# Two-layer hybrid attention backbone: load order at the start, modulation pace, kept output parts and late C heads

## The chip, the core and the metric

The kernel runs on one core of one Trainium2 chip. The metric is the device time of one execution in microseconds. The engines are TensorE (PE, whose weight loads are listed as PEld), VectorE (DVE), ScalarE (ACT), GpSimd (POOL) and SyncE (SP). Nearly all transfers are issued from SP's queue; ScalarE issues none, and GpSimd issues some small ones. The whole program is planned at build time: each engine gets one fixed list of instructions, with semaphores between the engines.

## The reference

Two layers work on 512 latent tokens `x` and 256 context tokens `ctx`, with a model width D of 2048, all in float32. In each layer (cut to what matters):

```python
shift, scale, gate = split(silu(c) @ w_ada[l] + b_ada[l], 3)          # and the same with c_ctx for ctx
h  = rms(x,  norm_w[l]) * (1 + scale)   + shift
hc = rms(xc, norm_w[l]) * (1 + scale_c) + shift_c
u  = h @ w_in[l]          # queries, keys, values of A and B; low-rank cq, ckv, kpe of C; gate path z
o_a = neighbourhood attention, 8 heads of 64, over latent neighbours and all context keys
o_b = sliding-window grouped attention, 12 query heads, 4 kv heads of 64, with sinks and rotary
o_c = latent attention, 6 heads of 128 + 64, over all 768 keys
y   = concat(o_a, o_b, o_c) * silu(z)
x   = x + gate * (y @ w_out[l])
# layer 0 alone: xc = xc + gate_c * (y_c @ w_out[l]), where context reads context only
```

The output is `x` after the second layer.

## The kernel before

**Precision and tiles.** Every float32 operand of a data matmul is split in a high part (float32r) and a low rest, and three products are made: high by high, high by low, low by high. The splitter (L394) does it for weights: a ScalarE copy to `wh`, then a VectorE subtraction to `wl`. `hilo` (L343) does it for activations. There are 3 buffers of `ws` (weights as loaded), 3 of `wh`, 2 of `wl`, 6 PSUM banks `g`, one double bank `S`, 5 buffers `tm`, and 52 buffers `s3` of 128 x 768 (named `s` in the profile) for nearly everything else.

**The planner.** Strands of work are Python generators (fibers) with priorities. `Weaver.run` (L111) runs them against a virtual clock, with a cost for each instruction (L230 to L337), and so fixes the order of each engine's list. `main` goes through a list of jobs; a `TJob` (L437) or `FJob` (L538) makes one output tile column by pieces of weights, and spawns a `post` strand that empties its PSUM banks. A job with `fine` waits for its inputs slice by slice (128 rows of K, called k). A `Group` deals the pieces of several jobs by turns. A strand that needs an event or a buffer that is not there yields to others.

**The start.** `load_x` (L874) loads the rows of x and of ctx as 24 tiles of 128 x 512 from SP's queue: for each of four column blocks, four of x, then two of ctx. `use_x` and `turn_x` square and transpose them. `ada_blocks` (L724) then streams the shift and scale columns of `w_ada` of layer 0 through PE; after its first eight loads it sets `ev_go`, with which the weight loader begins. The first eight loads are the shift and scale columns of k = 0. `make_hk` (L951) forms h for slice k as soon as its shift and scale are there. Layer 0's first jobs are `kv` and `q` of four A heads, their K halved by `HALF`, in one Group.

**The rest of modulation.** All other modulation vectors (gate of layer 0, shift, scale and gate of layer 1) are made on VectorE by `ada_vec` (L784): for each slice of 128 x 512 of `w_ada`, loaded to one of two `wa` buffers, one multiply-add into `ac` for each of latent and context (L266), then a small PE reduction. After each slice the strand sleeps `PACE[stage[0]]` planner microseconds (L814): 5.5 at first, 2.0 from the last C weight job of layer 0 on (`stage` 1, L2124), 10.0 from layer 1 on. Gate 0 and layer 1's shift and scale are 192 slices of two products; gate 1 is 64 slices of one. The gates go to DRAM (`gscr`) and come back as rows, one for all partitions.

**Order in a layer.** A heads, B heads, then the C heads, mixed with jobs of z and of the low-rank parts; attention units (scores, softmax, transposes, value product) are run by two worker strands beside the jobs. The C heads come last, in the order of `ORDER_C`. A head's gated output is stored to DRAM (`yscr`) and, by `load_y` (L1939) and `load_one` (L1950), loaded back and split for the output projection; L1939 waits until enough `s3` buffers are free.

**Output projection.** The first `CUT` output columns blocks of 256 (3 in layer 0, 2 in layer 1) are cut in K: a job over k = 0 to 13 whose result is kept by `post_part` (L1965), and later a finishing job over k = 14 and 15 whose `post_out` (L1978) adds the kept part, multiplies by the gate, adds the residual x, and in layer 0 also squares for the next norm. The other columns are one job each, the later ones 512 wide; in layer 1 `post_out` then multiplies, adds and stores to the output.

Of the kernel before, what the change touches and what calls it, by code (L numbers as in the profile page):

```python
# [21 lines left out]
D = 2048  # L22
# [19 lines left out]

HALF = 8
# [4 lines left out]
PACE = [5.5, 2.0, 10.0]  # L48
# [91 lines left out]
class Kern:  # L140
# [296 lines left out]
class TJob:  # L437


    def __init__(self, K, W, runs, nk, tiles, lhs, evs, post, room=None, kpp=2, after=None, k0=0):  # L440
        self.after, self.np, self.k0 = after, nk // kpp, k0
        self.K, self.W, self.runs, self.nk, self.tiles, self.kpp = K, W, runs, nk, tiles, kpp
        self.lhs, self.evs, self.post, self.room = lhs, evs, post, room
        self.wd = sum(n for _, n in runs)
        m = 512 // self.wd
        self.banks = [tiles[i:i + m] for i in range(0, len(tiles), m)]
        self.ps = [None] * len(self.banks)
        self.done = [Event() for _ in self.banks]
        self.inS = self.fine = False

    def specs(self):
        n, m = self.wd, self.kpp

        def mk(p):
# [8 lines left out]
            return dict(load=load, kind="split", cols=m * n)  # L463
# [168 lines left out]
def body(K):  # L632
# [241 lines left out]
    def load_x():  # L874

        for c in range(4):
            st = []
            for i in range(6):
                x = yield from K.get("s3")
                w.cur.ft = w.vt  # L880
                src = t["x"][0, i * 128:(i + 1) * 128] if i < 4 else t["ctx"][0, i * 128 - 512:i * 128 - 384]
                tx = yield from K.load_ahead(x[:, :512], src[:, c * 512:(c + 1) * 512])
                st.append((x, tx))
            w.spawn(use_x(c, st), 0)

    def use_x(c, st):
        left = [4, 4]
        for k in range(4 * c, 4 * c + 4):
            xk[k] = yield from K.get("s3")
        for k in range(4 * c, 4 * c + 4):  # L890
            for seg in range(2):
                w.spawn(turn_x(k, seg, st, left), 1)
        sq = yield from K.get("s3")
        for i, (x, tx) in enumerate(st):
# [3 lines left out]
        for e in ev_x[c]:  # L898
            K.set(e)

    def turn_x(k, seg, st, left):
        a, b = SEG[seg]
        w.cur.ft = max(tx for _, tx in st[a:b])
# [8 lines left out]
        if left[seg] == 0:  # L912
            K.put("s3", *(x for x, _ in st[a:b]))
# [496 lines left out]
    def layer(l):  # L1410
# [473 lines left out]
        def attend_C(h):  # L1884
# [54 lines left out]
        def load_y():  # L1939
            for f in range(KT):  # L1940
# [4 lines left out]
                s = yield from K.get("s3", n=3)  # L1945
                hi, lo = K.take("s3", F32R), K.take("s3", F32R)
# [3 lines left out]
        def load_one(f, s, hi, lo):  # L1950
            yield from K.load(s[:, :ntok], yscr[f], 512 * ntok)
# [12 lines left out]

        def post_part(n):  # L1965

            def gen(ps, done):
                for b in range(len(qt) // 2):
# [3 lines left out]
                    K.put("g", ps[b])  # L1972
                    K.set(ev_part[n, b])
            return gen
# [3 lines left out]
        def post_out(c0, wd, tiles):  # L1978
# [8 lines left out]
            def gen(ps, done):  # L1987
# [3 lines left out]
                gs, tg, xin = {}, 0.0, []  # L1991
                for x in sides:
                    if x == 0 or wd > 256 or 0 not in sides:
                        g = yield from K.get("tm")
                    gs[x] = (g, 256 * x if wd == 256 else 0)
                    ga = gscr[l][x]
                    yield from K.load(g[:, gs[x][1]:gs[x][1] + wd], bass.AP(tensor=ga.tensor, offset=ga.offset + c0, ap=[[0, 128], [1, wd]]),
                           512 * wd)
# [10 lines left out]
                for b, ts in enumerate(banks):  # L2009
                    yield from K.wait(done[b])  # L2010
                    xt, tx = xin[b] if early else ((yield from K.get("tm")), None)
# [3 lines left out]
                    w.cur.ft = w.vt  # L2015
                    r = slice(ts[0] % 4 * 128, ts[0] % 4 * 128 + 128 * m)
                    if not early:
                        if ts[0] < 4:
                            src = (xs1 if last else t["x"][0])[r, cols]
                        else:  # L2020
                            src = t["ctx"][0, r, cols]
                        yield from K.load(xv, src.rearrange("(t p) n -> p t n", p=128))
                        tx = w.cur.ft
                    w.cur.ft = max(done[b].t, tg)
                    src = ps[b]
                    if (c0 // 256, b) in part:
                        yield from K.wait(ev_part[c0 // 256, b])
                        yield from K.add(o, src, part[c0 // 256, b][:, :512])
                        K.put("s3", part[c0 // 256, b])
                        src = o  # L2030
                    g, ga = gs[int(ts[0] >= 4)]
                    yield from K.mul(ov, src.rearrange("p (t n) -> p t n", n=wd),
                          g[:, None, ga:ga + wd].to_broadcast([128, m, wd]))
# [9 lines left out]
                    K.put("s3" if early else "tm", xt)  # L2043
# [33 lines left out]
        if cut:  # L2077
# [4 lines left out]
            jobs.extend([Group([kv[0], q[0]]), Group(zs), Group([kv[1], q[1]]), zjob(0)])  # L2082
# [23 lines left out]
        jobs[-1].after = free_h  # L2106
        J(lambda: w.spawn(free_B(), 1))
# [15 lines left out]
        if l == 0:  # L2123
            J(lambda: stage.__setitem__(0, 1))  # L2124
        J(lambda: free_c("kv", 4))

        def free_y(kpp):
# [3 lines left out]
            return fn  # L2131

# [6 lines left out]
        while c0 < D:  # L2139
            wd = 512 if c0 % 512 == 0 else 256  # L2140
            final = c0 + wd == D
            for tiles in ([lat, cx] if final and not last else [qt]):
# [3 lines left out]
                jobs.append(TJob(K, t["w_out"][l], [(c0, wd)], KT, tiles, lhs_y, ev_yT, post_out(c0, wd, tiles), kpp=kpp,  # L2146
                                 after=free_y(kpp) if final and tiles[-1] == qt[-1] else None))
                jobs[-1].inS = wd == 512 and tiles is not cx
            c0 += wd
# [48 lines left out]
    def ada_rest():  # L2198
# [3 lines left out]
        stage[0] = 2  # L2202
# [72 lines left out]
```

## Time and profile before

| | us |
|---|---|
| runs of the kernel before | 2886.25, 2877.25, 2882.88 |
| their median | 2882.88 |
| the profiled execution's own time | 2875.56 |
| its span, first to last instruction | 2873.8 |

The mean granted TensorE clock of the profiled execution is 0.992. The profile is of one execution, with times counted from the span's start. Windows give each engine's busy time in a stretch; a tile is named by the program's name for it. L233 is every ScalarE activation, L239 every VectorE two-tensor instruction, L266 every VectorE scalar-tensor-tensor instruction, L277 the softmax maximum, L308 every load and store from SP's queue, L338 every data matmul and L341 every transpose, because helpers record them; so groups are told apart by their tiles. PE idle time between matmuls is listed with the engine that ended it.

### The profile page before, as it was taken

The numbers are of one execution on the slowest core, as the hardware profiler recorded it, in microseconds if no ns is written. First come the engines' busy times: TensorE is split into PE (matmuls) and PEld (weight loads), VectorE is DVE, ScalarE is ACT, GpSimd is POOL, SyncE is SP. The second block draws the span as 40 slices with busy tenths as digits, with TensorE's granted clock in tenths as the row PEclk, the third lists the DMA queues.
The fourth block names the chain that finished last, engine by engine and source line by source line (L and its number), as shares of the span: only waits on it lengthen the run. The fifth ranks groups of instructions, "written<-read, shape, count | busy, mean of one in ns | idle before, by whom it ended". The sixth has DMA issues, their size and how long they took to land.

```text
span 2873.8 us, 51646 instructions
## 1 busy us (share of the span) xinstructions
PE 2774.4 (97%) x19270; PEld 2610.4 (91%) x19270; DVE 1985.4 (69%) x5088; ACT 1209.1 (42%) x2656; POOL 147.9 (5%) x217
## 2 busy tenths in 40 slices
PE   7999999999999999899999999999999999999998
PEld 5789999999999999889988779999999888889977
DVE  4347776757897688989873485656667867599643
ACT  3323434434444354556321273433334545466421
POOL 2000000000011001000000000000001000000000
PEclk8999999999999999999999999999999999999999
DMA  9853434333233334325353443333333333413253
GB/s 291 281 166 105 120 92 121 107 103 111 86 99 102 107 111 144 100 81 165 113 169 103 137 149 107 109 105 107 109 107 92 103 115 111 120 46 97 85 177 117
DMA packets 388428, 349.93 MB, mean 122 GB/s; under 512 B 47876, under 2 KB 315954, under 8 KB 388176
## 3 DMA queue, kind: packets, MB, share of 16 engines
q1 hardware_dynamic: 386304, 345.31, 40.2%
q0 software_dynamic: 1872, 1.32, 0.5%
q8 instruction: 151, 2.47, 0.4%
q14 instruction: 101, 0.83, 0.1%
HBM read 305.01 MB, written 32.07 MB: 117 GB/s over the span
## 4 chain that ended last, share of the span: by engine, by line
PE 82%; DVE 10%; DMA 3%; issue 2%; ACT 2%; SPq 1%; DVEq 0%; ACTq 0%
PE g L338 65%; PE S L338 10%; PE g L341 5%; DVE s L239 2%; DVE wl L239 1%; DVE s L266 1%; DVE s L277 1%; PE g L761 1%; DVE ac L266 1%; ACT s L233 1%; PE g L819 1%; DVE tm L239 1%; DVE s L261 1%; DVE pt L239 1%; SPq L308 1%
## 5 line engine op out<-in xcount | busy, mean ns | idle before, releaser
L338 PE MATMUL g<-wh,s 128*128 128x256 f32 (+2 forms) x6248 | 1304.4, 297 | 21.9 <-DVE tm L239 5.6
L338 PEld LDWEIGHTS g<-wh,s 128*128 128x128 f32 x6248 | 1022.8, 192 | 50.1 <-ACT s L233 9.6
L338 PE MATMUL g<-wl,s 128*128 128x256 f32 (+2 forms) x3124 | 920.8, 295 | 5.7 <-DVE wl L239 5.2
L338 PE MATMUL g<-s,wh 128*128 128x384 f32 (+1 forms) x2688 | 762.2, 354 | 1.2 <-ACT s L233 0.8
L239 DVE TENSOR_TENSOR wl<-ws,wh 128x512 fp32r<-128x512 f32 (+1 forms) x606 | 418.2, 690 | 496.0 <-PE g L338 273.2
L338 PEld LDWEIGHTS g<-wl,s 128*128 128x128 f32 x3124 | 599.0, 192 | 20.6 <-DVE wl L239 11.2
L233 ACT ACTIVATE wh<-ws 128x512 fp32r<-128x512 f32 (+2 forms) x614 | 377.6, 616 | 437.3 <-PE g L338 357.0
L338 PEld LDWEIGHTS g<-s,wh 128*128 128x128 f32 x2688 | 492.1, 188 | 31.2 <-issue 2.1
L338 PE MATMUL g<-s,wl 128*128 128x384 f32 (+1 forms) x1280 | 448.2, 350 | 0.3 <-DVE wl L239 0.3
L233 ACT ACTIVATE s<-s,sm 128x512 f32<-128x512 f32 (+3 forms) x260 | 192.5, 740 | 453.8 <-DVE sm L277 369.9
L266 DVE SCALAR_TENSOR_TENSOR ac<-wa,scT,ac 128x512 f32<-128x512 f32 x420 | 307.9, 753 | 5.4 <-DMA wa<-w_ada 4.9
L338 PEld LDWEIGHTS g<-s,wl 128*128 128x128 f32 x1280 | 240.9, 188 | 12.4 <-DVE wl L239 0.6
L341 PE MATMUL g<-ident,s 128*128 128x128 f32 x1488 | 225.4, 279 | 22.8 <-DMA s<-x 6.8
L338 PE MATMUL S<-s,s 128*128 128x256 f32 (+3 forms) x1260 | 233.1, 313 | 12.4 <-DVE sm L277 6.2
L239 DVE TENSOR_TENSOR pt<-g,pt 128x512 fp32r<-128x512 f32 (+1 forms) x306 | 187.2, 622 | 42.6 <-ACT pt L233 40.7
L338 PE MATMUL g<-pt,s 128*128 128x256 f32 (+1 forms) x1348 | 208.4, 285 | 8.2 <-DVE pt L239 5.6
L338 PEld LDWEIGHTS S<-s,s 128*128 128x128 f32 x1260 | 187.6, 189 | 29.8 <-DVE sm L277 12.5
L233 ACT ACTIVATE pt<-g 128x512 fp32r<-128x512 f32 (+1 forms) x306 | 160.1, 542 | 120.4 <-PE g L341 116.2
L341 PEld LDWEIGHTS g<-ident,s 128*128 128x128 f32 x1488 | 176.6, 143 | 35.6 <-issue 8.4
L233 ACT ACTIVATE tm<-g 128x384 f32<-128x384 f32 (+4 forms) x240 | 113.4, 491 | 205.5 <-PE g L338 131.3
L338 PEld LDWEIGHTS g<-pt,s 128*128 128x128 f32 x1348 | 184.5, 191 | 14.5 <-DVE pt L239 8.9
L287 POOL TENSOR_TENSOR s<-ot,s 64x256 f32<-64x256 f32 x100 | 88.1, 881 | 1467.5 <-DVE ot L239 1328.6
(163 smaller groups left out, 2429.3 us busy)
## 6 DMA issues: line engine op xcount, KB each, us to landing
ws<-w_in SPq DMA_DIRECT2D x288, 256.0 KB
wa<-w_ada SPq DMA_DIRECT2D x256, 256.0 KB
ws<-w_out SPq DMA_DIRECT2D x144, 256.0 KB
s<-w_ada SPq DMA_DIRECT2D x128, 256.0 KB
ws<-w_in SPq DMA_DIRECT2D x200, 128.0 KB
s<-scr SPq DMA_DIRECT2D x36, 384.0 KB
ws<-w_qb SPq DMA_DIRECT2D x54, 192.0 KB
s<-scr SPq DMA_DIRECT2D x40, 256.0 KB
```

What stands on the lines that cost most here:

```text
L233: self.nc.scalar.activation(out, in_, func, bias=bias, scale=scale, **kw)
L239: self.nc.vector.tensor_tensor(out, a, b, op=op)
L261: self.nc.vector.tensor_scalar(out, a, s1, s2, op0=op0, op1=op1)
L266: self.nc.vector.scalar_tensor_tensor(out, a, s, b, op0=op0, op1=op1)
L277: self.nc.vector.tensor_tensor_reduce(out, a, b, -1.0, init, OP.add, OP.min, acc)
L287: self.nc.gpsimd.tensor_tensor(out, a, b, op=OP.mult)
L308: self.nc.sync.dma_start(out, in_)
L338: self.nc.tensor.matmul(out, l, r, start=start, stop=stop, skip_group_check=True)
L341: self.nc.tensor.transpose(out, in_, self.ident)
L761: nc.tensor.matmul(ps[j:j + 32, :n], scT[:, kk, :], s[:, x * n:(x + 1) * n], start=kk < 4, stop=kk >= 12, skip_group_check=True)
L819: nc.tensor.matmul(pt[:, 2 * c + m:2 * c + m + 1], a[:, c * 128:(c + 1) * 128], one, start=c == 0 and m == sides[0], stop=c == n // 128 - ...
```

## The change

Six edits are made together.

1. `load_x` loads all 16 tiles of x first. The 8 tiles of ctx wait for `ev_go`, that is for the issue of the first eight modulation loads. `use_x` and `turn_x` work per segment.
2. The first Group of layer 0 has q ahead of kv.
3. The paces become 4.0, 25.0, 2.0 and 10.0 by stage. The new stage 1 begins after the last z job of layer 0, before the C heads; stage 2 begins where stage 1 did; stage 3 is layer 1.
4. C heads with y tile 12 or above (`STAY`) keep their gated output in its buffer; `load_one` splits it from there, with no store and reload.
5. `post_part` multiplies its bank by the gate row and adds the residual when it keeps it; the finishing job's `post_out` then multiplies its own bank by the gate and adds the kept part as its residual.
6. The last output job of layer 1 has its weights multiplied by the gate row in the splitter; `post_out` then only adds and stores. The gate row is loaded by a strand spawned one job ahead.

```diff
-PACE = [5.5, 2.0, 10.0]
+STAY = 12
+PACE = [4.0, 25.0, 2.0, 10.0]
...
 def splitter(self):
+            if sp.get("gate"):
+                yield from self.wait(sp["gate"][1])
+                yield from self.mul(s, s, sp["gate"][0][0])
...
 def load_x():
-        for c in range(4):
-            st = []
-            for i in range(6):
+        for seg in range(2):
+            for c in range(4):
+                if seg:
+                    yield from K.wait(ev_go)
+                st = {}
+                for i in range(*SEG[seg]):
...
 def attend_C(h), use():
-                    yield from K.store(yscr[f], sz[f][:, :ntok], 512 * ntok)
-                    K.put("s3", sz[f])
+                    if f < STAY:
+                        yield from K.store(yscr[f], sz[f][:, :ntok], 512 * ntok)
+                        K.put("s3", sz[f])
...
 def load_y():
-                s = yield from K.get("s3", n=3)
-                hi, lo = K.take("s3", F32R), K.take("s3", F32R)
+                s = (yield from K.get("s3", n=3)) if f < STAY else sz[f]
+                hi = yield from K.get("s3", F32R, n=2)
+                lo = K.take("s3", F32R)
 def load_one(f, s, hi, lo):
-            yield from K.load(s[:, :ntok], yscr[f], 512 * ntok)
+            if f < STAY:
+                yield from K.load(s[:, :ntok], yscr[f], 512 * ntok)
+            else:
+                yield from K.wait(ev_y[f])
...
 def post_part(n), gen(ps, done):
+                yield from K.wait(ev_gate[l])
+                gs = yield from gates(n * 256, 256, range(1 if last else 2))
                 for b in range(len(qt) // 2):
                     yield from K.wait(done[b])
+                    xt = yield from K.get("tm")
+                    yield from K.load(xv, residual(n * 256, 256, [2 * b, 2 * b + 1]))
                     part[n, b] = yield from K.get("s3")
-                    yield from K.act(part[n, b][:, :512], ps[b])
+                    yield from K.mul(o, ps[b], gate row)
                     K.put("g", ps[b])
+                    yield from K.add(o, o, xt)
...
 def post_out(c0, wd, tiles, gated=False), gen(ps, done):
-                    if (c0 // 256, b) in part:
-                        yield from K.add(o, src, part[c0 // 256, b][:, :512])
-                    yield from K.mul(ov, src, gate row)
-                    K.put("g", ps[b])
+                    if not gated:
+                        yield from K.mul(ov, sv, gate row)
+                        K.put("g", ps[b])
+                        sv = ov
                     if last:
-                        yield from K.add(ov, ov, xv)
+                        yield from K.add(ov, sv, xv)
...
-            jobs.extend([Group([kv[0], q[0]]), Group(zs), Group([kv[1], q[1]]), zjob(0)])
+            jobs.extend([Group([q[0], kv[0]]), Group(zs), Group([kv[1], q[1]]), zjob(0)])
...
         for f in range(10 if last else 13, KT):
             jobs.append(zjob(f))
+        if l == 0:
+            J(lambda: stage.__setitem__(0, 1))
...
-            J(lambda: stage.__setitem__(0, 1))
+            J(lambda: stage.__setitem__(0, 2))
...
+                gated = final and last
+                if gated:
+                    jobs.insert(len(jobs) - 1, Call(lambda: w.spawn(load_g(), 1)))
+                    jobs[-1].gate = (gl, ev_gl)
```

In the diff, `gate row` stands for the broadcast slice of the gate tile, and `xv` is the kept part in a finishing job.

More of the change, by code (lines that the diff above doesn't have):

```diff
@@ L448, in __init__ @@
         self.done = [Event() for _ in self.banks]
+        self.gate = None
         self.inS = self.fine = False
@@ L462, in load @@
                     off += wd
-            return dict(load=load, kind="split", cols=m * n)
+            return dict(load=load, kind="split", cols=m * n, gate=self.gate)
         return [mk(p) for p in range(self.nk // m)]
@@ L874, in load_x, with use_x @@
     def load_x():
-        for c in range(4):
-            st = []
-            for i in range(6):
[L879 to L886, printed above, removed]
+        for seg in range(2):
[4 more added lines that the diff above has]
+                for i in range(*SEG[seg]):
+                    x = yield from K.get("s3")
+                    w.cur.ft = w.vt
+                    src = t["ctx"][0, i * 128 - 512:i * 128 - 384] if seg else t["x"][0, i * 128:(i + 1) * 128]
+                    tx = yield from K.load_ahead(x[:, :512], src[:, c * 512:(c + 1) * 512])
+                    st[i] = (x, tx)
+                w.spawn(use_x(c, seg, st), 0)
+    def use_x(c, seg, st):
         left = [4, 4]
         for k in range(4 * c, 4 * c + 4):
[L889 to L892, printed above, removed]
+            if seg == 0:
+                xk[k] = yield from K.get("s3")
+            w.spawn(turn_x(k, seg, st, left), 1)
         sq = yield from K.get("s3")
-        for i, (x, tx) in enumerate(st):
+        for i, (x, tx) in st.items():
             w.cur.ft = max(w.vt, tx)
@@ L912, in turn_x @@
         if left[seg] == 0:
[L913 removed]
+            K.put("s3", *(x for x, _ in st.values()))
         yield from K.copy(xk[k][:, a * 128:b * 128], ps[:, :(b - a) * 128])
@@ L1963, in layer, with residual, gates @@
         part = {}
+        def residual(c0, wd, ts):
+            r = slice(ts[0] % 4 * 128, ts[0] % 4 * 128 + 128 * len(ts))
+            src = t["ctx"][0] if ts[0] >= 4 else xs1 if last else t["x"][0]
+            return src[r, c0:c0 + wd].rearrange("(t p) n -> p t n", p=128)
+        def gates(c0, wd, sides):
+            gs = {}
+            for x in sides:
+                if x == 0 or wd > 256 or 0 not in sides:
+                    g = yield from K.get("tm")
+                gs[x] = (g, 256 * x if wd == 256 else 0)
+                ga = gscr[l][x]
+                yield from K.load(g[:, gs[x][1]:gs[x][1] + wd], bass.AP(tensor=ga.tensor, offset=ga.offset + c0, ap=[[0, 128], [1, wd]]),
+                       512 * wd)
+            return gs
@@ L1990, in gen @@
                 w.cur.ft = w.vt
[L1991 to L1998, printed above, removed]
+                xin = []
+                gs = {} if gated else (yield from gates(c0, wd, sides))
                 tg = w.cur.ft
@@ L2010, in gen @@
                     yield from K.wait(done[b])
-                    xt, tx = xin[b] if early else ((yield from K.get("tm")), None)
+                    cut = part.get((c0 // 256, b)) if wd == 256 else None
+                    if cut is not None:
+                        xt = cut
+                    else:
+                        xt, tx = xin[b] if early else ((yield from K.get("tm")), None)
                     o = yield from K.get("tm")
@@ L2015, in gen @@
                     w.cur.ft = w.vt
-                    r = slice(ts[0] % 4 * 128, ts[0] % 4 * 128 + 128 * m)
[L2017 to L2023, printed above, removed]
-                    w.cur.ft = max(done[b].t, tg)
-                    src = ps[b]
-                    if (c0 // 256, b) in part:
-                        yield from K.wait(ev_part[c0 // 256, b])
-                        yield from K.add(o, src, part[c0 // 256, b][:, :512])
[L2029 to L2033, printed above, removed]
-                    K.put("g", ps[b])
+                    if cut is not None:
+                        yield from K.wait(ev_part[c0 // 256, b])
+                        tx = w.cur.ft
+                    elif not early:
+                        yield from K.load(xv, residual(c0, wd, ts))
+                        tx = w.cur.ft
+                    r = slice(ts[0] % 4 * 128, ts[0] % 4 * 128 + 128 * m)
+                    w.cur.ft = max(done[b].t, tg)
+                    sv = ps[b].rearrange("p (t n) -> p t n", n=wd)
+                    if not gated:
+                        g, ga = gs[int(ts[0] >= 4)]
+                        yield from K.mul(ov, sv, g[:, None, ga:ga + wd].to_broadcast([128, m, wd]))
+                        K.put("g", ps[b])
+                        sv = ov
                     w.cur.ft = max(w.cur.ft, tx)
                     if last:
-                        yield from K.add(ov, ov, xv)
+                        yield from K.add(ov, sv, xv)
+                        if gated:
+                            K.put("g", ps[b])
                         yield from K.store(t["out"][0, r, cols].rearrange("(t p) n -> p t n", p=128), ov)
@@ L2042, in gen @@
                                   ov[:, :, kk * 128:(kk + 1) * 128], xv[:, :, kk * 128:(kk + 1) * 128])
-                    K.put("s3" if early else "tm", xt)
+                    K.put("s3" if early or cut is not None else "tm", xt)
                     K.put("tm", o)
@@ L2131, in free_y, with load_g @@
             return fn
+        gl, ev_gl = [], Event()
+        def load_g():
+            yield from K.wait(ev_gate[l])
+            g = yield from K.get("s3")
+            ga = gscr[l][0]
+            yield from K.load(g[:, :512], bass.AP(tensor=ga.tensor, offset=ga.offset + D - 512, ap=[[0, 128], [1, 512]]))
+            gl.append(g[:, :512])
+            K.set(ev_gl)
         cut = CUT[l]
@@ L2201, in ada_rest @@
         yield from K.wait(*(e for p in ev_in[1] for e in p))
-        stage[0] = 2
+        stage[0] = 3
         yield from ada_gate(1)
```

24 lines of the change are left out of this document (19 added, 5 removed).

## Prediction

> **What bounds the kernel now.** I read the page first, then busy time by windows of the stages, then who TensorE (PE) waited for in the worst stages, then the order of time at both ends.
>
> ```profile
> span 2873.8 us, 51646 instructions
> PE 2774.4 (97%) x19270; PEld 2610.4 (91%) x19270; DVE 1985.4 (69%) x5088; ACT 1209.1 (42%) x2656; POOL 147.9 (5%) x217
> PE 82%; DVE 10%; DMA 3%; issue 2%; ACT 2%; SPq 1%; DVEq 0%; ACTq 0%
> ```
>
> PE is busy 97% and makes 82% of the chain that ended last. No matmul on data is removed here, so only PE's gaps, 2873.8 - 2774.4 = 99 us of them, can be won, and a little at the end. Where they lie (columns: window, its length, PE, PEld, DVE, ACT, POOL busy, granted clock, DMA share, GB/s):
>
> ```profile
> core 0: us, PE busy (x) PEld busy (x) DVE busy (x) ACT busy (x) POOL busy (x), PEclk, DMA share, GB/s
> 0.00:50.00 50.00, 31.31 (x255) 24.48 (x255) 26.03 (x81) 23.07 (x65) 19.46 (x41) 0.83 1.01 269
> 50.00:150.00 100.00, 93.68 (x850) 76.59 (x851) 34.98 (x73) 27.62 (x54) 1.72 (x3) 0.97 0.94 298
> 250.00:1100.00 850.00, 841.41 (x6097) 833.18 (x6096) 647.34 (x1708) 358.75 (x836) 64.77 (x81) 1.00 0.35 104
> 750.00:850.00 100.00, 96.15 (x745) 94.48 (x744) 91.35 (x254) 49.00 (x126) 12.15 (x13) 1.00 0.28 82
> 1100.00:1350.00 250.00, 228.94 (x1567) 216.51 (x1566) 226.31 (x643) 143.21 (x331) 12.11 (x20) 0.99 0.39 119
> 1450.00:1510.00 60.00, 53.12 (x427) 52.19 (x426) 43.99 (x73) 12.09 (x19) 0.00 (x0) 0.97 0.54 164
> 2400.00:2650.00 250.00, 243.88 (x1586) 224.79 (x1586) 198.72 (x578) 142.71 (x326) 5.95 (x6) 1.00 0.32 95
> ```
>
> Three places lose: the start (DMA full, 18.7 us idle in 50), the C heads of layer 0 (1100 to 1350: 21.1 us idle, DVE busy 226 of 250), and the cut output jobs of layer 0 (1450 to 1510: 6.9 us). The C heads of layer 1 (2400 to 2650) do the like with 6.1 us idle. What differs is the modulation, whose products of w_ada tiles (wa) sit on DVE (same columns, only instructions on wa, so DVE alone):
>
> ```profile
> 150.00:1100.00 950.00, 186.00 (x260) 1.00 0.37 109
> 1100.00:1350.00 250.00, 37.05 (x51) 0.99 0.39 119
> 1350.00:1510.00 160.00, 51.46 (x73) 0.99 0.47 147
> ```
>
> One k-slice is two such instructions. To 1100 the planner's pace of 5.5 gave 130 slices in 950 us, 7.3 us each, so 1.8 us over the pace. 384 instructions make gate 0 and all layer-1 vectors: 260 + 51 + 73.
>
> **New paces (4 / 25 / 2 / 10).** At 4.0 plus the same 1.8 a slice takes 5.8 us: 950 / 5.8 = 164 slices by 1100, 34 more than now. These are 68 instructions at 37.05 / 51 = 0.73 us, 50 us of DVE that move from 1100 to 1510 into the A and B stages. Beside C a slice comes every 25 + 1.8 us: 9 slices, 13 us of DVE instead of 37. The 19 slices left run at the old stage's 160 x 2 / 73 = 4.4 us, 84 us, and end near 1430.
>
> C of layer 0 gets 24 us of DVE back. Who is waited for there, then one row of C in layer 1, then the DMA queue in C of layer 0 (us in total, times, longest):
>
> ```profile
> PE g L338 <- DVE pt L239: 4.6, 4, 1.8
> PE g L338 <- DVE wl L239: 4.0, 5, 1.7
> PE g L338 <- ACT wh L233: 2.3, 1, 2.3
> PE S L338 <- DVE sm L277: 2.0, 3, 1.1
> SPq L308 <- DVE ac L266: 12.4, 4, 7.1
> ```
>
> The long waits are for DVE, and SP's queue stands 12.4 us behind wa tiles, with weight loads (ws) queued behind them. With the pause both shrink. The gain is at least about 0 (if gaps are chain latency) and at most 33.5 us, the idle time of the weight-load row (250 - 216.51). I take layer 1's C, the nearest row with no modulation: 2.4% idle; 228.94 / 0.976 = 234.5, so **-16**. DVE then needs 226 - 24 = 202 of 234, 86%, against layer 1's 79%: near enough. Low end of the gain 4, high end 30.
>
> A and B pay: DVE goes from 647 to about 693 of 850 (82%). PE idles 8.6 us there now. The stretch 750 to 850 shows the price of a full DVE: 91% busy, 3.9 us idle in 100. If four further stretches of 100 us come to that, each 3 us worse than the mean of 1, it costs 12; if DVE's slack hides all, 0. The one such stretch that there is lies among eight, and 50 us spread over 850 bring one or two more there: **+4**, ends 0 and 12. The wait queued behind it is the splitter's lo part (wl) and the softmax, which stand behind the two products on DVE.
>
> [...]
>
> **Start.** The eight ctx loads move behind the first eight modulation loads, and q's weights go before kv's. DMA queue, then PE, then the ctx size:
>
> ```profile
> 19.92 2.90 SPq L308 DMA_DIRECT2D s<-ctx  x2
> 22.87 9.54 SPq L308 DMA_DIRECT2D s<-w_ada  x8
> 36.07 5.09 SPq L308 DMA_DIRECT2D s<-w_ada  x7
> 43.36 0.38 PE L338 MATMUL g<-wh,s 128*128 128x256 f32 x1 [1.99 <-ACT s L233]
> 51.10 0.58 PE L338 MATMUL g<-wh,s 128*128 128x256 f32 x1 [1.99 <-ACT s L233]
> s<-ctx SPq DMA_DIRECT2D x8, 256.0 KB
> ```
>
> 2 MB at 269 to 298 GB/s is 7 to 8 us: the first shift and scale columns, and the first projection matmul at 43.36, come that much sooner. But they serve k = 0 alone; the next eight modulation loads now stand behind ctx, so k = 1 (51.10) stays where it is, as the bytes ahead of it are the same. PE's program is in order and bank 0 of the first piece needs k = 1 after six matmuls. Only those and some transposes leave the busy region, so **-2**, ends -8 (all of it) and +3 (ctx late for bank 2 of q, the ctx transposes then beside projections). What is late next is k = 1's modulation, DMA-bound.
>
> **Kept parts.** In layer 0, 3 jobs x 3 banks. Before: ACT copies the part; later DVE adds part, multiplies by the gate, adds x. After: DVE multiplies and adds x when kept, later it multiplies and adds. Waits at 1450 to 1510, DVE groups there, and the ACT copy at 1340 to 1460:
>
> ```profile
> PE g L338 <- DVE tm L239: 5.6, 3, 2.4
> PE g L819 <- DVE tm L239: 1.1, 1, 1.1
> L266 DVE SCALAR_TENSOR_TENSOR ac<-wa,scT,ac 128x512 f32<-128x512 f32 x30 | 21.3, 748 | 3.5 <-DMA wa<-w_ada 3.3
> L239 DVE TENSOR_TENSOR s<-tm 128x256 f32<-128x256 f32 x14 | 5.5, 419 | 1.1 <-DMA tm<-x 1.1
> L239 DVE TENSOR_TENSOR tm<-tm 128x512 f32<-128x512 f32 x7 | 4.8, 689 | 0.2
> L239 DVE TENSOR_TENSOR tm<-g,s 128x512 f32<-128x512 f32 x7 | 4.8, 688 | 0.1
> L271 DVE TENSOR_REDUCE ssx<-s 128x6 f32<-128x768 f32 x3 | 2.8, 944 | 0.0
> L233 ACT ACTIVATE s<-g 128x512 f32<-128x512 f32 x6 | 3.6, 596 | 10.6 <-PE g L338 10.6
> ```
>
> PE waits there for PSUM banks (g) that DVE has not read. A finishing job costs DVE 3 x (0.688 + 0.689 + 2 x 0.419) + 2 x 0.944 = 8.5 us, beside 43% modulation; after, 3 x (0.689 + 0.838) + 1.9 = 6.5 us, the bank is freed by the first instruction, and modulation is over. Of 5.6 + 1.1 = 6.7 us I take **-6**, ends 0 and -7. Early, the parts add 9 x 1.38 = 12 us to DVE, which loses 17 slices there (25 us): nothing, as long as modulation ends by 1450. The product now waits for the gate row and holds its bank meanwhile; the gate's 64 slices are done near 150 + 64 x 5.8 = 521, so only its load can be late, with the softmax of the last heads queued behind it on DVE: 1 or 2 us, in the ends. Nine residual loads and six gate loads go earlier on SP's queue, beside DMA at half load: 0. Layer 1 (4 banks, no modulation, 0 to -2): 0.
>
> The eviction moves from ACT (596 ns) to DVE (688 ns, the same as the 689 ns of an SBUF source). [...]
>
> **Late heads of C on chip.** Four y tiles per layer skip a store and a reload; the loads of y, first and last:
>
> ```profile
> 1306.92 1.46 SPq L308 DMA_DIRECT2D s<-scr  x3
> 1360.32 0.32 SPq L308 DMA_DIRECT2D s<-scr  x1
> ```
>
> The last is needed only by the finishing jobs near 1480, so its trip is hidden: 0. The held tiles take up to four of 52 buffers; that loads began at once after q's buffers fell free says there was room. Ends -3 (less queueing) and +6 (a head's room waits).
>
> **The end.** Layer 1's last job has its weights multiplied by the gate in the splitter: 16 x 0.69 us on DVE, and only an add behind the last matmul.
>
> ```profile
> 2867.17 0.40 PE L338 MATMUL g<-wh,s 128*128 128x512 f32 x1
> 2864.47 0.69 DVE L239 TENSOR_TENSOR tm<-S,tm 128x512 f32<-128x512 f32 x1 [2.88 <-PE S L338]
> 2867.55 0.68 DVE L239 TENSOR_TENSOR tm<-g,tm 128x512 f32<-128x512 f32 x1
> 2869.60 0.69 DVE L239 TENSOR_TENSOR tm<-tm,s 128x512 f32<-128x512 f32 x1
> 2865.91 4.74 SPq L308 DMA_DIRECT2D out_dram<-tm  x4
> ```
>
> DVE ends at 2870.3, 2.7 us behind PE's last matmul, since four banks bring eight instructions. With four, the last add starts some 0.7 us after that matmul's end at 2867.6 at the latest and ends by 2868.4 to 2869: **-2**, ends -1 and -2.2. The products hide beside matmuls: DVE idles 2.88 us before the first row, waiting for PE, and one product fits there. The splitter waits for the gate row, with its own later pieces and the weight buffers behind it; the row is loaded a job ahead. Without that cover the products cost 16 x 0.69 = 11.
>
> **Sum.** -2 + 4 - 16 - 6 + 0 - 2 = -22. The profiled execution took 2875.56 (span 2873.8), so it would be 2853.6; the median of the runs, 2882.88, is 7.3 above it, so I forecast 2882.88 - 22 = **2861**.
>
> **Rivals.**
> 1. C's gaps are latency (softmax chain, split chain), not DVE's load. For it: layer 1's C idles too. Against: DVE at 91%. C gives 4: -10, **2873**. Chance 0.14.
> 2. C nearly closes: 30 instead of 16, as SP's blocking goes too: -36, **2847**. 0.15.
> 3. Slower: DVE becomes the bound in A and B. It decides from about 90% busy; the new mean is 82%. If two thirds of the 850 us run at C's present 8.4% idle, that is 48 us against 6 now, +42 in place of +4: +16, **2899**. For it: 750 to 850 is at 91% already. Against: that stretch idles only 3.9%. 0.08.
> 4. The pace does nothing in A and B (slices stay at 7.3 us, bound by queue or DVE): A and B cost 0, 62 slices are left, 9 go beside C, and 53 x 4.4 = 233 us reach past the cut jobs, so their 6 are lost: -20, **2863**. 0.05.
>
> My forecast has 0.58. What a measurement can tell from no change is 0.3%, 8.6 us. Faster: 0.54 of my case, rivals 2 and 4, half of rival 1, 0.81; within: the rest of both, 0.12; slower 0.07. The range, 2840 to 2879, holds the forecast with the ends of C, A and B, and rivals 1, 2 and 4.
>
> **What would show it.** Right: in 1100 to 1350 under 20 wa instructions, PE idle under 10 us, DVE under 90%; no wa instruction after 1450; no waits on tm at the cut jobs; first projection matmul near 36 but k = 1 near 50; four adds at the end. Wrong: PE idle in 250 to 1100 above 20 us, or PE idle in C still near 20 with DVE lighter.

## The result, and the profile after

The changed kernel takes **2865.72 us** in the median of 4 runs (2865.18 to 2867.86), beside 2883.7 for the kernel before (4 runs, 2877.25 to 2886.25): ratio 0.9948, 95% interval 0.9935 to 0.9961, so 15 us faster by the ratio and 17 below the median that the forecast of 2861 set out from. The sign came out, and two thirds to three quarters of the forecast 22; of the terms behind the size, not all did.

The profiled execution after took 2865.18 us, close to its median. That of before took 2875.56, 7 to 8 below its own: the two traces differ by 10.4 us, and what they are short of the timing lies in no trace.

The page after, its head and the shares of the chain:

```profile
span 2863.4 us, 51590 instructions
PE 2776.1 (97%) x19270; PEld 2616.3 (91%) x19270; DVE 1997.8 (70%) x5113; ACT 1199.0 (42%) x2643; POOL 148.8 (5%) x217
PE 83%; DVE 10%; DMA 3%; issue 2%; ACT 1%; SPq 1%; DVEq 0%; ACTq 0%
```

TensorE still bounds the kernel, with 12 us less idle (2863.4 - 2776.1 = 87 instead of 99). The same windows as in the prediction, with the same columns, after the change:

```profile
0.00:50.00 50.00, 30.63 (x259) 24.02 (x260) 28.45 (x83) 23.69 (x67) 19.51 (x41) 0.86 0.97 281
50.00:150.00 100.00, 96.14 (x876) 79.07 (x876) 35.39 (x76) 26.87 (x53) 1.76 (x3) 0.97 0.96 298
250.00:1100.00 850.00, 837.57 (x6049) 829.05 (x6048) 671.69 (x1728) 350.42 (x824) 67.57 (x81) 0.99 0.38 112
750.00:850.00 100.00, 92.83 (x704) 90.87 (x703) 88.48 (x248) 47.44 (x125) 12.57 (x12) 0.93 0.29 87
1100.00:1350.00 250.00, 236.54 (x1611) 227.00 (x1610) 224.13 (x656) 149.25 (x347) 11.12 (x20) 0.97 0.36 108
1450.00:1510.00 60.00, 59.89 (x500) 59.68 (x499) 30.48 (x54) 13.14 (x20) 0.00 (x0) 1.00 0.41 118
2400.00:2650.00 250.00, 244.28 (x1615) 225.81 (x1614) 203.14 (x581) 145.91 (x333) 4.18 (x5) 1.00 0.30 92
```

C of layer 0 has PE busy 236.5 instead of 228.9, the cut jobs 59.9 instead of 53.1 of 60. The stretch 750 to 850 went the other way: 92.8 instead of 96.2, and the clock fell from 1.00 to 0.93. In C the clock fell too, from 0.99 to 0.97. Windows at fixed times hold slightly different work in the two kernels, so I also use a **lead**: the trace lists every matmul, and adding up their durations at full clock in order gives the work done at each moment; the lead is how much earlier the changed kernel has done the same work. It comes out so, in us (time in the kernel before, lead there):

| 142 | 807 | 861 | 1113 | 1343 | 1446 | 1505 | 2693 | 2745 | 2850 | end |
|---|---|---|---|---|---|---|---|---|---|---|
| +3.0 | +3.5 | -6.3 | -6.0 | +3.8 | +0.8 | +9.7 | +12.4 | +7.2 | +8.8 | +10.4 |

So the start won 3, one place near 815 lost 10, C won 10, the stretch behind it gave 3 back, the cut jobs won 9, layer 1's cut jobs lost 5 and the end won 3. A lead is read from one execution each: in e1, a second run of the same program, the place near 815 lost 7.5, C won 8 and the end stands at +7.3. A single term is thus good to 2 or 3 us.

**The loss near 815.** Waits of PE in 750 to 850 (total, times, longest), the longest before and then after; after the change, PE's rows and DVE's around the wait; then three windows:

```profile
PE g L338 <- DVE pt L239: 1.6, 1, 1.6
PE S L340 <- DVE sm L279: 4.7, 2, 4.1
814.81 0.74 PE L340 MATMUL S<-s,s 128*128 128x256 f32 x4
819.68 1.43 PE L340 MATMUL S<-s,s 128*128 128x384 f32 x4 [4.13 <-DVE sm L279]
814.26 0.48 DVE L279 CUSTOM_DVE_ANT_0 s<-S,zero,sm 128x256 f32<-128x256 f32 x1
819.14 0.48 DVE L279 CUSTOM_DVE_ANT_0 s<-S,zero,sm 128x256 f32<-128x256 f32 x1
800.00:820.00 20.00, 15.87 (x131) 15.63 (x131) 17.05 (x39) 9.22 (x20) 2.27 (x2) 0.94 0.38 112
820.00:840.00 20.00, 17.79 (x103) 16.69 (x103) 14.98 (x45) 10.73 (x34) 1.71 (x2) 0.72 0.18 54
818.00:828.00 10.00, 6.11 (x23) 5.01 (x24) 7.78 (x22) 3.39 (x10) 0.00 (x0) 0.50 0.26 80
```

One matmul waits 4.13 us for a softmax maximum (L279), and the clock then is at 0.50 for 10 us and averages 0.72 over 20 us. From the end of one maximum (814.74) to the end of the next (819.62) DVE takes 4.9 us, with one modulation product of 0.75 us in between, right behind the first maximum. PE's list has no other matmul between these two groups of score products, so it stands idle for most of that chain. The wait costs 4, the lost clock (1 - 0.72) x 20 + (1 - 0.94) x 20 = 6.8 more, together 11, where the lead shows 10. A wait of 4.1 us stands there in every run with the pace of 4.0 (one number, seen in eight profiles), and in none with 4.7 or 5.5.

**The loss in layer 1's cut jobs.** The window 2700 to 2760 before, then after, then the timeline after (SPq is a DMA issue):

```profile
2700.00:2760.00 60.00, 59.13 (x366) 52.89 (x366) 29.24 (x51) 18.48 (x32) 0.00 (x0) 1.00 0.50 152
2700.00:2760.00 60.00, 56.09 (x303) 48.74 (x302) 23.18 (x36) 14.01 (x23) 0.00 (x0) 0.94 0.44 132
2716.33 0.39 SPq L310 DMA_DIRECT2D out_dram<-tm  x1
2720.88 0.69 DVE L241 TENSOR_TENSOR tm<-g,tm 128x512 f32<-128x512 f32 x1 [3.81 <-DMA out_dram<-tm]
2722.69 0.68 DVE L241 TENSOR_TENSOR wl<-ws,wh 128x512 fp32r<-128x512 f32 x1
2723.42 0.80 PE L340 MATMUL S<-wl,s 128*128 128x512 f32 x1 [3.91 <-DVE wl L241]
```

A product with the gate waits 3.81 us for its output tile, because the tile's last content is still on its way to DRAM; the splitter's lo half stands behind it on DVE, PE 3.91 us behind that, and the clock falls: to 0.50 in the 5 us behind that wait (2723.4 to 2728.4), to 0.94 over the 60 us. The parts gated early take tm tiles (five in all) for gate rows and residual rows just before the finishing jobs want theirs; that this is why a tile with an open store comes up here, and not in the kernel before, is my reading of the program and not measured.

### The profile page after: what moved, and what is told of

The parts are those of the page before. It is cut to its first block, busy times and chain, and to the rows that moved or that the text cites. A ratio compares the mean times of both kernels' runs of the same rounds, so it can differ in the third digit from the quotient of the medians.

```text
span 2863.4 us, 51590 instructions
## 1 busy us (share of the span) xinstructions
PE 2776.1 (97%) x19270; PEld 2616.3 (91%) x19270; DVE 1997.8 (70%) x5113; ACT 1199.0 (42%) x2643; POOL 148.8 (5%) x217
## 4 chain that ended last, share of the span: by engine, by line
PE 83%; DVE 10%; DMA 3%; issue 2%; ACT 1%; SPq 1%; DVEq 0%; ACTq 0%
PE g L340 66%; PE S L340 10%; PE g L343 5%; DVE wl L241 1%; DVE s L268 1%; DVE s L241 1%; SPq L310 1%; DVE s L279 1%; DVE tm L241 1%; PE g L825 1%; DVE ac L268 1%; ACT s L235 1%; PE g L767 1%; DVE pt L241 1%; DMA s<-w_ada 1%
## 5 line engine op out<-in xcount | busy, mean ns | idle before, releaser
L340 PEld LDWEIGHTS g<-wl,s 128*128 128x128 f32 x3124 | 599.1, 192 | 21.1 <-DVE wl L241 12.2
L235 ACT ACTIVATE tm<-g 128x384 f32<-128x384 f32 (+3 forms) x240 | 113.0, 490 | 201.6 <-PE g L340 136.3
```

The costliest lines, as they stand in the source:

```text
L235: self.nc.scalar.activation(out, in_, func, bias=bias, scale=scale, **kw)
L340: self.nc.tensor.matmul(out, l, r, start=start, stop=stop, skip_group_check=True)
```

## The experiments

The kernel before had medians of 2882 to 2884 beside them. Intervals are 0.0012 to 0.0016 to either side, some 4 us, so differences of 2 or 3 us between runs settle nothing by themselves, and 5 us barely.

| run | median us | ratio to before | 95% interval |
|---|---|---|---|
| e1, the changed kernel again | 2868.14 | 0.9947 | 0.9935 to 0.9959 |
| e2, old pace | 2867.77 | 0.9950 | 0.9938 to 0.9962 |
| e3, pause only | 2870.51 | 0.9956 | 0.9943 to 0.9968 |
| e4, fast pace only | 2865.2 | 0.9940 | 0.9928 to 0.9951 |
| e5, late heads as before | 2868.55 | 0.9946 | 0.9932 to 0.9960 |
| e6, start as before | 2870.36 | 0.9954 | 0.9943 to 0.9966 |
| e7, last job not gated in its weights | 2872.81 | 0.9964 | 0.9951 to 0.9977 |
| e8, layer 1's parts as before | 2864.22 | 0.9930 | 0.9914 to 0.9946 |
| e9, store from the kept part | 2862.45 | 0.9926 | 0.9913 to 0.9939 |
| e10, e9 with pace 4.7 | 2852.58 | 0.9893 | 0.9879 to 0.9907 |
| e11, layer 0's gated parts alone | 2874.18 | 0.9966 | 0.9952 to 0.9979 |
| e12, e10 without the pause | 2861.55 | 0.9927 | 0.9913 to 0.9941 |

**The paces, e1 to e4.** e1 is the changed kernel itself.

> The changed kernel itself, to see what of its profile comes again. My theory: its one long PE wait in the B stage (4.1 us at 815 us, for the softmax maximum on DVE) and the half clock behind it (0.72 from 820 to 840 us) follow from the order of DVE's list, and so come again, as do the 3.9 us wait near 2718 us and the clock dip behind it; median 2863 to 2869 us. Rival: the clock dips are an accident of one execution; then PE's clock from 800 to 850 us is 1.00 here and the span is 5 to 8 us shorter.

It came out with the same wait of 4.1 us and a clock of 0.95 in 750 to 850, and the same loss near 2718: PE waits 4.1 us there, and the clock is 0.94 over 2700 to 2760. Both waits belong to the program.

```diff
-PACE = [4.0, 25.0, 2.0, 10.0]
+PACE = [5.5, 5.5, 2.0, 10.0]     # e2
+PACE = [5.5, 25.0, 2.0, 10.0]    # e3
+PACE = [4.0, 4.0, 2.0, 10.0]     # e4
```

> Paces of before (5.5 up to the output jobs, then 2.0), all other edits kept. My theory (DVE load decides): A and B get back about 10 us (PE idle 250 to 1100 under 10 us), C loses about 11 (PE idle 1100 to 1350 near 21 us again), the cut jobs lose 5 to 7 since modulation runs beside them; median 2870 to 2876 us. Rival (the paces only shuffle the order, the gain is from the other edits): 2863 to 2868 us.

> Old pace 5.5 before C, pause (25) beside C, then 2.0. My theory: A and B get back about 10 us, C keeps its gain (PE idle 1100 to 1350 near 13 us), but some 53 slices are left behind C, at 4.4 us each about 230 us, so they lie beside the cut jobs and those wait again for tm (5 to 7 us): 2860 to 2866 us. Rival (the cut jobs gain by the gated parts, not by the end of modulation): no waits on tm at the cut jobs, 2853 to 2858 us.

> Pace 4.0 up to and in C, no pause. A and B are the same as in the changed kernel, with the same long wait. My theory: the 28 slices left at 1100 us take 5.8 us each, 160 of C's 250 us, so C loses about two thirds of its gain, 6 to 8 us: 2871 to 2875 us. Rival (C's gaps are latency, not DVE's load): 2864 to 2868 us.

e2 and e4 came out where their rivals had them and not where my theory did (2870 to 2876, 2871 to 2875); e3 is above both of its ranges. The new paces as a whole are worth nothing that can be measured (e2 beside e1). Nor is the pause alone: at 4.0 the kernel without it (e4) is 3 us faster than e1, at 5.5 the one without it (e2) 3 us faster than e3, both within the noise. The window of C, and that of the cut jobs, in e2 and then e4:

```profile
1100.00:1350.00 250.00, 232.20 (x1592) 219.97 (x1591) 226.89 (x649) 145.18 (x340) 12.11 (x20) 0.99 0.38 115
1450.00:1510.00 60.00, 55.70 (x459) 54.89 (x458) 46.98 (x81) 11.99 (x18) 0.00 (x0) 1.00 0.56 164
1100.00:1350.00 250.00, 233.71 (x1623) 222.57 (x1622) 233.99 (x684) 146.83 (x341) 11.70 (x20) 1.00 0.39 119
1450.00:1510.00 60.00, 59.80 (x498) 59.60 (x498) 30.03 (x54) 12.52 (x19) 0.00 (x0) 1.00 0.41 114
```

The pause does take idle time out of C: PE idles 11.2 to 15.8 us of the 250 in the nine runs with it, and 16.3 to 21.1 in the five without, some 5 us more. But the changed kernel's 236.5 of 250 were at a clock of 0.97 and e4's 233.7 at 1.00, and (1 - 0.97) x 250 = 7.5 us is more than the 3 between them. By the lead from 1113 to 1446, C and the stretch behind it, the changed kernel wins 7 and e1 5, while e4 wins 10 without the pause.

The fast pace pays up to 10 near 815 (e4's lead falls from +5 to -4 there). With the old pace and the pause (e3) some 100 products are left behind C, but only 20 of them run after 1510: the lead falls from +16 at 1505 to +14 at 1600, and the further fall, to +5 at 2530, comes later.

**Parts undone one at a time, e5 to e8.**

```diff
-STAY = 12
+STAY = 16                                                   # e5
-jobs.extend([Group([q[0], kv[0]]), Group(zs), Group([kv[1], q[1]]), zjob(0)])
+jobs.extend([Group([kv[0], q[0]]), Group(zs), Group([kv[1], q[1]]), zjob(0)])   # e6, with load_x as before
-gated = final and last
+gated = False                                               # e7
+if PLAIN[l]:    # layer 1: ACT copies, add and gate later   # e8
```

> All of the change but one part: the late heads of C are stored and reloaded as before. The prediction put that part at 0 (the last y load is needed only near 1480): then 2866 us, within 2 of the changed kernel, and the waits at the cut output jobs stay as they are. Rival: part of the gain that the paces do not explain (the pace edit as a whole is worth about 0, so some 10 of 16 us are without an owner) comes from the four skipped trips: then 2870 or more, with PE idle growing between 1390 and 1510. Second rival: the held tiles crowd the buffers: then 2861 or less.

The ratio is e1's own, to 0.0001. The four trips were hidden; no term but 0 shows.

> All of the change but one part: ctx is loaded with x ahead of the modulation blocks, and kv's weights go before q's, as before. The prediction's term is -2 with ends -8 and +3; the profile shows a lead of 3 us over the kernel before at equal PE work by 85 to 140 us. By the first 2868, by the second 2869, with the first projection matmul back near 43 instead of 37.9 us. Rival: the start is worth the whole 5.5 us by which the first projection matmul came earlier: 2871 to 2872. If it does not show at all (2866), the lead at 140 us is given back in the DMA-bound stretch behind it.

0.0007 above e1, 2 us, less than the interval can tell; its lead at 142 us is +0.2 where the changed kernel has +3.0. The traces carry this term, the timing does not contradict it.

> All of the change but one part: the last output job is gated behind its matmuls again, not in its weights. The prediction's term is -2, and the profile has 2.7 us from the last matmul's start to the last DVE instruction's end fall to 1.1: so 2867.5, with eight DVE instructions at the end again. Rival: the 16 products on the weights in front of the splitter cost PE what they win at the end: 2866 or less.

0.0017 above e1, 5 us where 2 were forecast; neither the forecast nor the rival. In the profile the end makes 3.4 of it: from 2745 on the changed kernel's lead grows by 3.2 (7.2 to 10.4), that of e7, with eight instructions again, goes from 3.5 to 3.3. The rest is within the noise.

> All of the change but one part: in layer 1 the kept parts are copied by ACT and gated in the finishing jobs, as before; layer 0's are gated when kept. The prediction put layer 1's parts at 0, ends 0 and -2: so 2866 to 2868. Rival: the gated parts are what costs the 5 us that every variant loses at 2717 to 2729, where a DVE product waits 3.8 us for an output tile whose store has not landed, and TensorE's clock halves behind that: then 2861, and the granted clock stays at 1.00 there.

The rival holds by the trace. e8's window beside the 56.09 and 0.94 above:

```profile
2700.00:2760.00 60.00, 60.00 (x354) 53.47 (x353) 25.59 (x41) 17.13 (x29) 0.00 (x0) 1.00 0.51 147
```

No wait for out_dram is left, and PE is busy throughout. In the eight profiles with this edit as it was made (the changed kernel, e1 to e7) the lead falls by 3 to 6 us between 2693 and 2745; in e8 it does not. The ratio is 0.0017 lower, 5 us, which the two intervals alone do not tell apart. The edit for layer 1's parts was a loss inside a gain.

**Mending both losses, e9 and e10.** e9 lets the last add write into the kept part and stores from there, so the product's tile is free without a store; e10 also slows the pace.

```diff
-yield from K.add(ov, sv, xv)
+dst = xv if cut is not None else ov
+yield from K.add(dst, sv, xv)
+if cut is not None:
+    K.put("tm", o)                  # e9
-PACE = [4.0, 25.0, 2.0, 10.0]
+PACE = [4.7, 25.0, 2.0, 10.0]       # e10, with e9's edit
```

> The changed kernel with one thing more: in layer 1's cut output jobs the last add writes into the kept part and the store reads from there, so the product's tile (one of five tm buffers) is free at once instead of after the store. Theory: the 5 us lost near 2717 are a product that waits for a tile whose store has not landed, with the splitter's lo half and so PE behind it, and the half clock that follows. Then that wait is gone, the granted clock is 1.00 between 2700 and 2760, PE is busy 59 to 60 of those 60 us, and the time is 3 to 5 us below the changed kernel's 2866 to 2868: 2863, like the run with layer 1's parts as before. Rival: it is the earlier loads of residual rows and gate rows, which take tiles and queue time ahead of the finishing jobs; then the wait stays and the time too.

> The run before it in this call with a pace of 4.7 in place of 4.0 ahead of C. Theory: what A and B lose (9 us by 870) hangs on one wait of 4.1 us for a softmax maximum near 815, behind modulation products on DVE, and the half clock after it, and so on how products fall there; at 4.7 fewer products stand in the queue, the wait stays under 3.4 us and costs under 3, while C keeps what the pause brings: 6 us less than the run before it, 2857. Rival 1: the loss goes with DVE's load and only shrinks in proportion (half of 7 us): 2860. Rival 2: the wait is of the change's order of jobs and not of the pace: no difference, 2863. In either case some 45 products are left at 1350, twice the number of the run before it, which may cost 2 us at the cut jobs.

e9's window 2700 to 2760, then e10: the longest waits of PE in 750 to 850, the rows that match those near 815 above, that stretch and C:

```profile
2700.00:2760.00 60.00, 59.56 (x352) 52.40 (x351) 26.45 (x45) 15.90 (x29) 0.00 (x0) 1.00 0.44 131
PE S L340 <- DVE sm L279: 2.2, 2, 1.6
813.28 0.74 PE L340 MATMUL S<-s,s 128*128 128x256 f32 x4 [0.61 <-DVE sm L279]
817.99 0.85 PE L340 MATMUL S<-s,s 128*128 128x384 f32 x4
812.73 0.48 DVE L279 CUSTOM_DVE_ANT_0 s<-S,zero,sm 128x256 f32<-128x256 f32 x1
817.44 0.48 DVE L279 CUSTOM_DVE_ANT_0 s<-S,zero,sm 128x256 f32<-128x256 f32 x1
750.00:850.00 100.00, 97.40 (x750) 95.78 (x749) 88.77 (x243) 46.27 (x116) 15.78 (x13) 1.00 0.30 85
1100.00:1350.00 250.00, 238.81 (x1673) 227.14 (x1672) 229.85 (x665) 154.03 (x355) 12.02 (x20) 0.99 0.36 108
```

e9's wait for the store is gone, and 3 to 6 us with it; its rival, in which the wait stays, falls. At 4.7 the longest wait for the maximum is 1.6 us instead of 4.1 and the clock stays at 1.00, though DVE is busy 88.77 of 100 there, no less than the 88.48 at 4.0. So DVE's mean load does not decide, and rival 1 falls. My theory had the wrong reason, though: the chain did not get shorter with fewer products ahead of it. It takes 4.7 us between the same two maxima (813.21 to 817.92) beside 4.9, with one modulation product in it as before. What differs is PE's list, which at 4.7 has projection matmuls and transposes from 813.86 to 817.92 between the two score products, where at 4.0 it has none. The pace changes the order that the planner gives every engine; why it comes out so at 4.0 no run shows. Nor does any show that 3.4 us, the bound that I set for the wait, is where its price changes: the wait left here is 1.6 us, and one of 1.9 us in C had a lower clock behind it in two of eight profiles (last section).

It went further than my theory's 2857: e10, at 2852.6, is the fastest of all, 31 us below the kernel before.

**Layer 0's parts alone, e11.** The kernel before with that one edit.

> The kernel before with one part of the change alone: layer 0's kept parts gated and added to x when kept; paces, start, late heads, layer 1's parts and last job as before. The prediction gave the cut jobs -6 for this and for modulation being over by then. By the curves of the runs with slower paces, 5 us of lead come in between 1390 and 1500 while modulation still runs there: so 5 less than the kernel before, 2878, with PE busy 55 to 56 of 60 in 1450 to 1510 instead of 53. Rival: the gain there needs modulation to be over; then 2882 to 2884. If the parts made while modulation is at its most crowded cost PE, it shows between 1340 and 1450.

```profile
1450.00:1510.00 60.00, 58.01 (x483) 57.61 (x482) 50.16 (x86) 13.35 (x20) 0.00 (x0) 1.00 0.64 188
```

10 us, more than the 5 I expected, and with modulation still running there (DVE 50 of 60). By the lead it is 6.8, from -1.9 at 1446 to +4.9 at 1505; its interval reaches from 6 to 14. By the median, this edit is most of the change's gain.

**The pause at 4.7, e12.**

```diff
-PACE = [4.7, 25.0, 2.0, 10.0]
+PACE = [4.7, 4.7, 2.0, 10.0]
```

> The run with a pace of 4.7 and the store from the kept part, but with modulation going on at 4.7 beside C instead of pausing at 25. The prediction's largest term, -16, was for C freed of modulation. Theory: VectorE's load in C is what idles TensorE, so that the pause carries that term: without it PE is busy 232 to 234 of 250 in 1100 to 1350, as with the old pace, against 238.8; the cut jobs get 2 to 3 us back, because modulation is over by 1400; together 3 us or more above the run with the pause: 2855 to 2858. Rival: the pause moves nothing that lasts, since what is not done beside C is done behind it, and the gain at 4.7 is the absence of the long wait near 815 alone: 2852, within 1.5 of the run with the pause, with PE in C at 237 or more or with the cut jobs giving all of it back.

The modulation products (wa) of e10 and of e12 in C, then C and the cut jobs in e12, and its longest wait in C:

```profile
1100.00:1350.00 250.00, 16.12 (x21) 0.99 0.36 108
1100.00:1350.00 250.00, 39.89 (x54) 0.97 0.39 118
1100.00:1350.00 250.00, 230.53 (x1556) 217.17 (x1555) 231.88 (x662) 146.61 (x342) 11.87 (x20) 0.97 0.39 118
1450.00:1510.00 60.00, 60.00 (x501) 59.85 (x500) 30.01 (x54) 12.60 (x20) 0.00 (x0) 1.00 0.40 115
PE g L340 <- DVE pt L241: 6.8, 5, 3.6
```

With 54 products in C instead of 21, PE falls from 238.8 to 230.5 and the clock from 0.99 to 0.97; the median rises by 9 us, where my theory had 3 to 6. By the lead C wins 12.0 with the pause (+4.9 at 1113, +16.9 at 1343) and 1.3 without (+4.5, +5.8); up to 1446 the two part by some 4.5 more, and the cut jobs give 3.6 back (5.5 won with the pause, 9.1 without). So at 4.7 the pause is worth its place. That it is VectorE's load in C which makes the difference is not shown: e4, without the pause at 4.0, has 56 products there, a VectorE busy 233.99 of 250 and a clock of 1.00, and wins 7.5 by the lead at 1343. Its longest wait in C is 1.9 us; e12 has one of 3.6, with the clock at 0.83 over the 10 us around it.

## Why the prediction was right, and where it was not

**What bounds it.** PE's gaps in the three places and the end were where the time lay; no other engine took over (after the change PE is busy 97% of the span, DVE 70%).

**The paces.** 164 slices by 1100 were forecast; the trace has 328 products, two a slice, and after them 24 in C (18 forecast) and 32 up to 1450, with none between 1450 and 1510:

```profile
150.00:1100.00 950.00, 235.75 (x328) 0.99 0.39 116
1100.00:1350.00 250.00, 18.35 (x24) 0.97 0.36 108
1350.00:1510.00 160.00, 22.75 (x32) 1.00 0.37 109
```

**C, -16.** Right in direction, too large, and the cause shown in part: -9.8 by the lead at 1343 in the changed kernel, of which 3 are gone again by 1446, and -12.0 in e10. The pause takes some 5 us of idle time out of C in every run that has it, but a gain in the timing is shown at 4.7 alone, where the medians of e10 and e12 differ by 9; at 4.0, the pace of this change, e4 does as well without it. Of the signs that the prediction set for C, fewer than 20 products (24) and under 10 us of idle time (13.5) failed, and VectorE under 90% was just met. Nor did the clock gain with the shorter gaps: it fell from 0.99 to 0.97. DVE did not fall to 202 of 234 but stayed at 224 of 250, 90%: C's other work closed up into what modulation left. PE's waits in C after are for the same names, fewer of them; the first three rows:

```profile
PE g L340 <- DVE wl L241: 4.8, 6, 1.9
PE g L340 <- DVE pt L241: 2.4, 2, 1.3
PE g L343 <- DVE pt L241: 2.0, 1, 2.0
```

So layer 1's C, with 79% on DVE, was too good a pattern. Rival 1 (chain latency) may hold part of the idle time; no run separates the two.

**A and B, +4.** This is the step that failed: about +10. I priced DVE's load by the idle time per 100 us of one crowded stretch, 3.9, and took the clock of 1.00 there as given. Load was not what changed there (DVE 91.35 before, 88.48 after): at one place PE's list had nothing to do beside a chain of 4.9 us on DVE, and with the lower clock behind it that cost as much as C won. With 4.7 and 34 more products before 1100 than in the kernel before (294 and 260), e10 loses nothing there. Rival 3 named this side but not this form: nothing near its 42 us, and decided by one wait, not by a mean of 90%. The prediction's sign for it, PE idle above 20 us in 250 to 1100, did not see it: the idle time rose from 8.6 to 12.4, and the rest went by the clock.

My sum had no term for a clock that falls where a gap opens. The traces have it: the clock was 0.50 from 818 to 828 us, where the wait of 4.13 us ends, and 0.50 for 5 us behind the wait of 3.91. In e5 the same wait of VectorE for the store (3.8 us) left PE only 2.5 us idle, and the clock stayed at 1.00 over the 60 us:

```profile
PE S L340 <- DVE wl L241: 2.5, 1, 2.5
2700.00:2760.00 60.00, 56.60 (x320) 49.31 (x319) 23.73 (x37) 14.12 (x23) 0.00 (x0) 1.00 0.48 142
```

**Cut jobs of layer 0, -6.** -8.9 by the lead, mis-sized. The window before had 6.9 us of idle time and a clock of 0.97; 0.03 x 60 = 1.8 us came back with the waits, 8.7 in all. No wait on tm is left.

**Layer 1's parts, 0.** Wrong: 5 us lost. I followed the earlier loads through SP's queue and the DMA engines but not the tiles: a finishing job's product stood for one whose store had not landed, and the loss goes when that tile needs no store (e9) or the parts are made as before (e8).

**Start, -2.** +3.0 of lead at 142 us, as forecast in kind: the first projection matmul comes early (43.36 before), k = 1 hardly does (51.10 before):

```profile
37.89 0.39 PE L340 MATMUL S<-wh,s 128*128 128x256 f32 x1 [2.90 <-ACT s L235]
48.80 0.39 PE L340 MATMUL S<-wh,s 128*128 128x256 f32 x1 [1.99 <-ACT s L235]
```

**The end, -2.** Four adds as forecast, and the last one ends at 2859.5, 1.1 us behind the last matmul's start instead of 3.1:

```profile
2858.40 0.39 PE L340 MATMUL g<-wh,s 128*128 128x512 f32 x1
2858.15 1.37 DVE L241 TENSOR_TENSOR tm<-g,s 128x512 f32<-128x512 f32 x2
```

That is 1.6 to 2; another 1.6 is won ahead of the last matmul (lead 7.2 to 8.8), so 3.2 in all.

**The sum.** By the lead: +3.5 - 9.8 + 0.3 + 9.8 - 3.0 + 8.9 + 2.7 - 5.2 + 3.2 = 10.4. By the ratios of the runs, in us: layer 0's parts 10, last job 5, start 2, late heads 0, paces 1, layer 1's parts -5: 13 of 15, with some 4 us to either side of each; the rest is less than the intervals tell. The traces thus show 11.6 less than the 22 of the forecast: 6 more lost in A and B, 5 lost in layer 1 and 6 too much in C, against 3 more at the cut jobs and some 3 more at the start and the end. The timing came nearer to the forecast than that, by the 7 us that the profiled execution of before lies below its median. That it fell so near is in part luck: the largest term, C with its pause, carries little of the measured gain at this pace, and layer 0's parts carry most of it. It stays open where the other executions of before lose those 7 us. Of the 3 given back between 1343 and 1446, some 1.7 are clock (0.57 granted from 1343 to 1347); the rest is open.

## What to carry to other kernels

Read the clock column with the idle column: a stretch's price is its idle time plus what the clock withholds (near 815 a wait of 4 us, and 6.8 of clock). Background work on a shared engine was not priced here by that engine's mean load (DVE busy 88.48 of 100 with the loss near 815, 88.77 without): look for places where the bound engine's list has nothing beside a chain on the shared one. A new pace re-plans every list, so try it in small steps (4.0 to 4.7 was worth 10 us, with DVE as busy as before in the crowded stretch), and test a pause at the pace that you keep. Where a step is moved ahead, follow each tile that the steps behind it want to the landing of the store that frees it (a wait of 3.81 us here).

## What the runs showed of the hardware

Behind a shorter wait the clock fell too. In C after the change the longest wait was 2.0 us, yet the clock fell: after a wait of 1.9 us at 1140.76 the next 10 us were granted 0.66 (the row gives PE busy 9.24 of 10).

```profile
1140.76 0.45 PE L340 MATMUL g<-wl,s 128*128 128x384 f32 x1 [1.90 <-DVE wl L241]
1140.00:1150.00 10.00, 9.24 (x39) 9.21 (x40) 5.30 (x17) 2.72 (x5) 6.75 (x13) 0.66 0.70 110
```

It was not always so. The same wait stands in all eight profiles with a pace of 4.0, at 1.88 to 1.91 us: in e5 the clock is 0.67 in the same window, in the six others it stays at 1.00 up to 1150, in e1 too, which is the same program:

```profile
1138.63 0.45 PE L340 MATMUL g<-wl,s 128*128 128x384 f32 x1 [1.90 <-DVE wl L241]
1135.00:1150.00 15.00, 12.88 (x75) 11.83 (x74) 10.26 (x25) 5.11 (x11) 8.06 (x15) 1.00 0.70 128
```

So with one length of wait the clock came out at 0.66 or 0.67 in two profiles and at 1.00 in six, and the length did not decide alone. Nor did the program; what did stays open. The price of a long wait varied as well: behind waits of 3.9 to 4.4 us near 2725 the clock over 2700 to 2760 was 0.94 in the changed kernel, e1, e3, e6 and e7, but 0.97 in e4, behind 4.3 us, and in e2, where PE is idle 3.96 of the 60 us.
